# Group 0's feed-forward in 512 columns, and one DRAM array for a head's queries, keys and decay rows

## The chip, the cores and the metric

The kernel runs on one core of a Trainium2 chip. The metric is device microseconds of one launch, the median of several runs. TensorE (PE in the profile) multiplies, with weight loads as a row of their own (PEld); VectorE (DVE), ScalarE (ACT) and GpSimd (POOL) do the elementwise work; SyncE (SP) issues nearly all DMA transfers, which run on the core's 16 DMA engines.

## The reference

One layer of a streaming encoder, for a prompt of 1024 frames and a running stream of 32 frames ("the sample"), D = 1024, all float32. Cut to what matters:

```python
h = x * (1 + sc1) + sh1                                  # modulated input, mod = silu(c) @ w_ada + b_ada
mq, mk, mv, mo, mi, mf, fq, fk, fv, ff, gu, gv = split(h @ w_in)
hm = mlstm(mq, mk, mv, li, lf)                           # 4 heads of 64, in chunks
logits = fq @ fk.T * 64**-0.5 + F[t] - F[s]              # fox: 8 heads of 64, F = cumsum(log_sigmoid(ff)), causal
hf = softmax(logits) @ fv
hg = gu * (tril(ws) @ layer_norm(gv) + bs)               # spatial gate, chunks of 128
x = layer_norm(ALPHA * x + (1 + g1) * (concat(hm, hf, hg) @ w_o))
h = x * (1 + sc2) + sh2
y = (silu(h @ w_gate) * (h @ w_up)) @ w_down             # feed-forward, 2816 wide
x = layer_norm(ALPHA * x + (1 + g2) * y)
```

The outputs are x, the fox keys, values and log-forgets, the mLSTM states and the sample's normed gv. The sample's fox attention also runs over 256 cached rows.

## The kernel before

Activations lie transposed, features on the partitions and frames in the free dimension. The 1056 frames make two groups: group 0 is frames 0 to 511, group 1 the other 512 and the 32 of the sample (544 columns). Each large product is done with both operands split into a high float32r part and a low rest: `gemm` issues three matmuls for each 128x128 block of weights (high x high, high x low, low x high). `weights` loads a block of 512 KB to `raw` (three buffers), rounds it on ACT to `whi` and subtracts on DVE to `wlo`.

`MM` cuts each group in two: 256 + 256 columns, and 272 + 272. `up(c, j, ...)` makes one of 22 blocks of 128 hidden features: for each cut, 24 matmuls for the gate and 24 for the up weights, SiLU, and the split into `acth` and `actl`. `down(c, g, ...)` adds a group of three or four such blocks (`GROUPS`) to the residual `z`; for each cut and each of 8 output blocks it runs 3 matmuls a hidden block and then `sublayer_end` on DVE. The layer-norm input to `up` lies in `hh` and `hl`, one tile a cut, made by `operand`.

The fox heads: `evac_qk(h)` takes the projection of one head, 64 query rows above 64 key rows, and stores its high and low parts to the DRAM arrays `dqh` and `dql`, [8, 128, 1056] each, once for each range of 256 or 272 columns. `gates` stores rows for the decay to `dfs` (8 partitions of 6 rows, 8 times). `fox(h, chunks)` then loads for one head `qp` (queries, high over low), `k1` (the high keys twice), `q2` (high queries over four decay rows), `k2` (low keys over four decay rows) and `v`, with nine loads:

```python
self.load(f(qp[0:64]), self.dqh[h, 0:64, qs])
self.load(f(qp[64:128]), self.dql[h, 0:64, qs])
self.load(f(k1[0:64]), self.dqh[h, 64:128, :nk])
self.load(f(k1[64:128]), self.dqh[h, 64:128, :nk])
...
```

`fox_chunk` takes query tiles of 128: two accumulating matmuls a bank of scores (`qp` with `k1`, `q2` with `k2`), maximum, exponential, division; then for each key block it transposes the probabilities to a PSUM bank, copies them to `pth` on ACT, subtracts to `ptl` on DVE, and multiplies both with `v`. `foxbufs` gives the number of buffers of `k1`, of `qp` and `q2`, of `k2` and of `v`: (2, 1, 1, 2) for group 0 and (2, 1, 1, 1) for group 1.

The order: projections with the fox heads and mLSTM blocks of group 0 between them (`ORDER`), the spatial gate, the output product and layer norm of group 0, the queries and keys of group 1 for the later heads, then `mixers` (fox on group 1 with query tiles 4 to 7, five mLSTM blocks after the heads of `MLB`, and the sample's fox at head `SAMP`), group 0's feed-forward, group 1's output product, and group 1's feed-forward, most of whose blocks run in `sup` with seven smaller products for eight. The program is written in that order, but a planner puts the instructions of each engine in order with a model of their times: it weaves the feed-forward of group 0 between the heads of `mixers`. On the chip each engine runs its own instructions strictly in the planned order.

Of the kernel before, what the change touches and what calls it, by code (L numbers as in the profile page):

```python
# [10 lines left out]
ALU = mybir.AluOpType  # L11
# [16 lines left out]
LN = MM  # L28
GROUPS = ((0, 3), (3, 3), (6, 4), (10, 4), (14, 4), (18, 4))
# [8 lines left out]
SAMP = 7  # L38
MLB = (1, 3, 5, 6, 7)
# [30 lines left out]
class Kernel:  # L70
# [288 lines left out]
    def evac_qk(self, h):  # L359
        nc = self.nc  # L360

        def evac(o, n, ps):
# [6 lines left out]
            self.store(self.dqh[h, :, o:o + n], f(hi[:, :n]))  # L369
            self.store(self.dql[h, :, o:o + n], f(lo[:, :n]))  # L370
# [15 lines left out]
    def gates(self):  # L386
# [47 lines left out]
        for j in range(8):  # L434
# [7 lines left out]
            self.store(self.dfs[:, :, j * P:(j + 1) * P], f(fr[64:72]))  # L442
# [214 lines left out]
    def fox(self, h, chunks):  # L657
# [26 lines left out]
    def fox_chunk(self, h, tiles, W, nq, k1, k2, qp, q2, v):  # L684
        nc, mx = self.nc, self.mx
        nb = tiles[-1] + 1
        t = lambda shape, dt, tag, bufs: self.t(mx, shape, dt, tag, bufs)
        probs = []
# [33 lines left out]

        o = self.t(self.po, [P, 512], F32, "o")
        full = tiles[0] + 1
        order = [0] + list(range(full, nb)) + list(range(1, full))
        held = None
        for x, b in enumerate(order):
            first = max(0, b - tiles[0])
            ps = self.t(self.pt, [P, 512], F32, "t")
            lo = first * P  # L730
            for y in range(first, len(tiles)):
                nc.tensor.transpose(ps[:, y * P:(y + 1) * P], probs[y][:, b * P:(b + 1) * P], self.ident)  # L732
            ph = t([P, max(nq, 384)], F32R, "pth", 3)
            pl = t([P, nq], F32R, "ptl", 2)
            nc.scalar.copy(ph[:, lo:nq], ps[:, lo:nq])  # L735
            nc.vector.tensor_tensor(pl[:, lo:nq], ps[:, lo:nq], f(ph[:, lo:nq]), ALU.subtract)  # L736
            nc.tensor.matmul(o[:, :nq] if b == 0 else o[0:64, lo:nq], v[:, b, :] if b == 0 else v[:, b, 0:64],
                             pl[:, lo:nq], start=b == 0, stop=False)
            if b == 0 and full == 1:
                held = ph  # L740
            else:
                nc.tensor.matmul(o[:, lo:nq], v[:, b, :], ph[:, lo:nq], start=False, stop=full > 1 and x == nb - 1)
            yield
            self.phase = "fox"
# [11 lines left out]
    def fox_sample(self):  # L756
# [29 lines left out]
        for g in range(2):  # L786
# [22 lines left out]
            pT = t([P, 3, P], "pth", 3)  # L809
# [81 lines left out]
    def operand(self, c, pool):  # L891

        new = lambda tag, n: self.t(pool, [P, KT * 272], F32R, tag, 1)[:, :KT * n].rearrange("p (k n) -> p k n", k=KT)
        self.hh[c], self.hl[c] = ({a: new(f"{x}{a}", b - a) for a, b in MM[c]} for x in ("ah", "al"))

    def wo_mix(self, c, ks):
        self.phase = f"wo{c}"
        nc = self.nc
        for a, b in MM[c]:
            for k in ks:  # L900
                r = self.t(self.p2, [P, 272], F32, "tmp", 4)[:, :b - a]
                self.load(r, self.dmix[c][:, k, a:b])
                nc.scalar.copy(self.hh[c][a][:, k], r)
                nc.vector.tensor_tensor(self.hl[c][a][:, k], r, f(self.hh[c][a][:, k]), ALU.subtract)
# [6 lines left out]
    def wo(self, c, st, cuts, eng, res=None):  # L911
# [6 lines left out]
        for m in range(KT):  # L918
# [5 lines left out]
            if m == 0:  # L924
                for i in range(KT):
                    for p, (a, b) in zip(ps, cuts):
                        self.gemm(p[:, :b - a], w[i:i + 1], slice(0, P), lambda _: hh[a][:, ko[i]],
                                  lambda _: hl[a][:, ko[i]], start=i == 0, stop=i == KT - 1)
            for p, (a, b) in zip(ps, cuts):
                if m:  # L930
                    self.gemm(p[:, :b - a], w, slice(0, P), lambda i: hh[a][:, ko[i]], lambda i: hl[a][:, ko[i]])
# [20 lines left out]
    def ln1(self, c, st, a, b):  # L952
# [3 lines left out]
        for k in range(KT):  # L956
# [11 lines left out]
            nc.scalar.copy(hh[:, k], h)  # L968
# [582 lines left out]
```

## Time and profile before

| | us |
|---|---|
| median of 3 runs (lowest, highest) | 1403.94 (1403.85, 1404.99) |
| the profiled execution, its own time | 1406.04 |
| its span, from the first to the last instruction | 1404.3 |
| PE busy / PEld busy | 1360.3 / 1310.1 |
| DVE busy / ACT busy / POOL busy | 1042.7 / 657.6 / 258.2 |

Busy times of PE are modelled, since matmuls are pipelined: the distance between starts tells more than the length of one. A line such as `L117 PE MATMUL up_g<-wo_ah,up_whi` names the line of the kernel (a helper's, here `gemm`), the engine, and the tiles written and read; the first part of a name is the phase in which the tile was made. `start_dqh` is the array `dqh`; `fox_k` stands for `k1` and `k2`, and `fox_q` for `q2`. The DMA share is the mean over the 16 DMA engines; it does not tell one from another.

### The profile page before, as it was taken

The numbers are of one execution on the slowest core, as the hardware profiler recorded it, in microseconds if no ns is written. First come the engines' busy times: TensorE is split into PE (matmuls) and PEld (weight loads), VectorE is DVE, ScalarE is ACT, GpSimd is POOL, SyncE is SP. The second block draws the span as 40 slices with busy tenths as digits, with TensorE's granted clock in tenths as the row PEclk, the third lists the DMA queues.
The fourth block names the chain that finished last, engine by engine and source line by source line (L and its number), as shares of the span: only waits on it lengthen the run. The fifth ranks groups of instructions, "written<-read, shape, count | busy, mean of one in ns | idle before, by whom it ended". The sixth has DMA issues, their size and how long they took to land.

```text
span 1404.3 us, 28827 instructions
## 1 busy us (share of the span) xinstructions
PE 1360.3 (97%) x10933; PEld 1310.1 (93%) x10933; DVE 1042.7 (74%) x2370; ACT 657.6 (47%) x1394; POOL 258.2 (18%) x299
## 2 busy tenths in 40 slices
PE   7999999999999899999999999999999999999996
PEld 4899988989889789999999999999999999999996
DVE  5548655668778768787787775577998989788777
ACT  3323234434445555555545454244663644445355
POOL 0103200042256600000000000353620000000331
PEclk9999999999999999999999999999999999999998
DMA  9754678475654576345443433655497667553321
GB/s 361 252 216 133 188 215 249 147 234 152 209 192 158 173 215 184 106 122 151 128 118 112 122 84 99 154 160 136 156 242 217 187 186 202 147 173 107 105 91 64
DMA packets 136386, 233.28 MB, mean 166 GB/s; under 512 B 22564, under 2 KB 79532, under 8 KB 136248
## 3 DMA queue, kind: packets, MB, share of 16 engines
q1 hardware_dynamic: 130936, 221.34, 50.5%
q0 software_dynamic: 5168, 9.96, 4.6%
q8 instruction: 86, 1.41, 0.4%
q14 instruction: 52, 0.43, 0.1%
q10 hardware_dynamic: 144, 0.14, 0.0%
HBM read 197.50 MB, written 53.81 MB: 179 GB/s over the span
## 4 chain that ended last, share of the span: by engine, by line
PE 81%; DMA 7%; DVE 7%; ACT 2%; issue 1%; SPq 1%; POOL 1%; DVEq 0%; ACTq 0%; POOLq 0%
PE up_g L118 5%; PE up_g L119 5%; PE up_g L117 5%; PE dn_g L117 4%; PE dn_g L118 4%; PE dn_g L119 4%; PE tm_g L282 3%; PE tm_g L283 3%; PE tm_g L284 3%; PE sup_u L119 3%; PE sup_u L117 3%; PE sup_u L118 3%; PE fox_t L732 2%; PE wo_g L118 2%; PE fm_g L117 2%; PE wo_g L117 2%
## 5 line engine op out<-in xcount | busy, mean ns | idle before, releaser
L117 PE MATMUL up_g<-wo_ah,up_whi 128*128 128x256 f32 (+1 forms) x704 | 200.6, 286 | 4.1 <-ACT lna_tmp L964 3.4
L118 PE MATMUL up_g<-wo_al,up_whi 128*128 128x256 f32 (+1 forms) x704 | 202.4, 288 | 0.6 <-DVE wo_al L969 0.6
L119 PE MATMUL up_g<-wo_ah,up_wlo 128*128 128x256 f32 (+1 forms) x704 | 200.9, 286 | 0.0
L117 PEld LDWEIGHTS up_g<-wo_ah,up_whi 128*128 128x128 f32 x704 | 133.3, 190 | 5.6 <-ACT lna_tmp L964 3.5
L118 PEld LDWEIGHTS up_g<-wo_al,up_whi 128*128 128x128 f32 x704 | 133.4, 190 | 1.4 <-DVE wo_al L969 0.8
L119 PEld LDWEIGHTS up_g<-wo_ah,up_wlo 128*128 128x128 f32 x704 | 133.6, 190 | 0.4 <-DVE up_wlo L106 0.2
L283 PE MATMUL tm_g<-tm_wlo,start_h1h 128*128 128x256 f32 (+1 forms) x384 | 111.2, 290 | 0.0
L284 PE MATMUL tm_g<-tm_whi,start_h1l 128*128 128x256 f32 (+1 forms) x384 | 110.9, 290 | 0.0
L282 PE MATMUL tm_g<-tm_whi,start_h1h 128*128 128x256 f32 (+1 forms) x384 | 110.3, 289 | 0.2 <-ACT tm_mixs L633 0.2
L117 PE MATMUL fm_g<-start_h1h,fm_whi 128*128 128x256 f32 (+2 forms) x344 | 101.9, 301 | 6.1 <-DVE fm_qkl L367 2.5
L118 PE MATMUL fm_g<-start_h1l,fm_whi 128*128 128x256 f32 (+2 forms) x344 | 101.8, 296 | 0.5 <-DVE start_h1l L223 0.5
L119 PE MATMUL fm_g<-start_h1h,fm_wlo 128*128 128x256 f32 (+2 forms) x344 | 100.8, 294 | 0.0
L117 PE MATMUL dn_g<-up_acth,dn_whi 128*128 128x256 f32 (+1 forms) x344 | 100.5, 293 | 0.0
L1088 ACT CAST sup_whi<-sup_raw 128x1024 fp32r<-128x1024 f32 x54 | 56.0, 1048 | 91.4 <-PE dn_u L118 47.8
L118 PE MATMUL dn_g<-up_actl,dn_whi 128*128 128x256 f32 (+1 forms) x344 | 98.7, 287 | 0.0
L119 PE MATMUL dn_g<-up_acth,dn_wlo 128*128 128x256 f32 (+1 forms) x344 | 98.5, 286 | 0.0
L735 ACT CAST fox_pth<-fox_t 128x256 fp32r<-128x256 f32 (+3 forms) x144 | 51.0, 373 | 65.7 <-PE fox_t L732 62.1
L1089 DVE TENSOR_TENSOR sup_wlo<-sup_raw,sup_whi 128x1024 fp32r<-128x1024 f32 x54 | 68.0, 1263 | 10.7 <-ACT sup_whi L1088 10.7
L282 PEld LDWEIGHTS tm_g<-tm_whi,start_h1h 128*128 128x128 f32 x384 | 73.5, 192 | 2.6 <-issue 1.6
L117 PEld LDWEIGHTS fm_g<-start_h1h,fm_whi 128*128 128x128 f32 x344 | 65.4, 192 | 11.3 <-DVE fm_qkl L367 3.2
L106 DVE TENSOR_TENSOR up_wlo<-up_raw,up_whi 128x1024 fp32r<-128x1024 f32 x50 | 63.3, 1265 | 16.5 <-ACT up_whi L105 16.2
L736 DVE TENSOR_TENSOR fox_ptl<-fox_t,fox_pth 128x256 fp32r<-128x256 f32 (+3 forms) x144 | 58.1, 417 | 22.6 <-ACT fox_pth L735 21.3
(577 smaller groups left out, 4678.9 us busy)
## 6 DMA issues: line engine op xcount, KB each, us to landing
up_raw<-w_gu SPq DMA_DIRECT2D x50, 512.0 KB
dn_raw<-w_dn SPq DMA_DIRECT2D x28, 512.0 KB
ada_late<-w_ada SPq DMA_DIRECT2D x24, 512.0 KB
wo_raw<-w_o SPq DMA_DIRECT2D x24, 512.0 KB
sup_raw<-w_gu SPq DMA_DIRECT2D x20, 512.0 KB
start_dp<-w_gu SPq DMA_DIRECT2D x19, 512.0 KB
start_dp<-w_gu POOLq DMA_DIRECT2D x19, 512.0 KB, 8.1
sup_raw<-start_dp SPq DMA_DIRECT2D x18, 512.0 KB
```

The lines of the kernel that those rows point to most:

```text
L106: (eng or nc.vector).tensor_tensor(lo[:, :w], raw[:, :w], f(hi[:, :w]), ALU.subtract)
L117: nc.tensor.matmul(ps, hi, xh(k), start=start and k == 0, stop=False)
L118: nc.tensor.matmul(ps, hi, xl(k), start=False, stop=False)
L119: nc.tensor.matmul(ps, lo, xh(k), start=False, stop=stop and k == n - 1)
L282: nc.tensor.matmul(ps[:, :ncol], xh, hi, start=k == 0, stop=False)
L283: nc.tensor.matmul(ps[:, :ncol], xh, lo, start=False, stop=False)
L284: nc.tensor.matmul(ps[:, :ncol], xl, hi, start=False, stop=k == 7)
L732: nc.tensor.transpose(ps[:, y * P:(y + 1) * P], probs[y][:, b * P:(b + 1) * P], self.ident)
L735: nc.scalar.copy(ph[:, lo:nq], ps[:, lo:nq])
L736: nc.vector.tensor_tensor(pl[:, lo:nq], ps[:, lo:nq], f(ph[:, lo:nq]), ALU.subtract)
L1088: nc.scalar.copy(h, x)
L1089: tt(l, x, f(h), ALU.subtract)
```

## The change

- Queries, keys and decay rows of a head go to one array `dq`, [8, 2, 2, 68, 1056]: head; queries or keys; high or low; 64 rows and four decay rows. `evac_qk` stores as before two transfers a range, and `gates` two where it stored one. `fox` loads `qp` in one transfer, `k1` in one (a broadcast), `q2` in one and `k2` in one, and `v`.
- `up` runs 512 columns at once for j = 1 to 17 of group 0, `down` for its first five groups. The operand of group 0 is one tile of 512 columns; the views for the cuts are taken from it.
- `fox_chunk` puts two key blocks in one bank, so that one copy and one subtraction serve both.
- `mixers` runs the sample's fox first, and weaves each mLSTM block with a head at half its pace; `MLB` is (1, 2, 3, 4, 5).

```diff
+WIDE = ((0, 512),)
...
-SAMP = 7
-MLB = (1, 3, 5, 6, 7)
+MLB = (1, 2, 3, 4, 5)
...
-            self.store(self.dqh[h, :, o:o + n], f(hi[:, :n]))
-            self.store(self.dql[h, :, o:o + n], f(lo[:, :n]))
+            for i, x in enumerate((hi, lo)):
+                self.store(self.dq[h, :, i, 0:64, o:o + n], f(x[:, :n]))
...
-            self.store(self.dfs[:, :, j * P:(j + 1) * P], f(fr[64:72]))
+            self.store(self.dq[:, 1, 1, 64:68, j * P:(j + 1) * P], f(fr[64:72, 0:4]))
+            self.store(self.dq[:, 0, 0, 64:68, j * P:(j + 1) * P], f(fr[64:72, 2:6]))
...
-        self.load(f(qp[0:64]), self.dqh[h, 0:64, qs])
-        self.load(f(qp[64:128]), self.dql[h, 0:64, qs])
-        self.load(f(k1[0:64]), self.dqh[h, 64:128, :nk])
-        self.load(f(k1[64:128]), self.dqh[h, 64:128, :nk])
-        self.load(f(q2[0:64]), self.dqh[h, 0:64, qs])
-        self.load(f(q2[64:68]), self.dfs[h, 2:6, qs])
-        self.load(f(k2[0:64]), self.dql[h, 64:128, :nk])
-        self.load(f(k2[64:68]), self.dfs[h, 0:4, :nk])
+        self.load(f(qp), self.dq[h, 0, :, 0:64, qs])
+        self.load(f(k1), self.dq[h, 1, 0:1, 0:64, :nk].to_broadcast([2, 64, nk]))
+        self.load(f(q2), self.dq[h, 0, 0, :, qs])
+        self.load(f(k2), self.dq[h, 1, 1, :, :nk])
         self.load(f(v), self.dv[:, :nb, h * P:(h + 1) * P])
...
+        units = [order[x:x + 2] for x in range(0, nb, 2)] if full > 1 else [[0], [1], [2, 3]]
...
-        for x, b in enumerate(order):
-            first = max(0, b - tiles[0])
+        for unit in units:
             ps = self.t(self.pt, [P, 512], F32, "t")
-            lo = first * P
-            for y in range(first, len(tiles)):
-                nc.tensor.transpose(ps[:, y * P:(y + 1) * P], probs[y][:, b * P:(b + 1) * P], self.ident)
-            ph = t([P, max(nq, 384)], F32R, "pth", 3)
-            pl = t([P, nq], F32R, "ptl", 2)
-            nc.scalar.copy(ph[:, lo:nq], ps[:, lo:nq])
-            nc.vector.tensor_tensor(pl[:, lo:nq], ps[:, lo:nq], f(ph[:, lo:nq]), ALU.subtract)
...
+            at, e = [], 0
+            for b in unit:
...
+                at.append((b, slice(e, e + w), slice(first * P, nq)))
+                e += w
+            ph = t([P, 512], F32R, "pth", b5)
+            pl = t([P, 512], F32R, "ptl", 2)
+            nc.scalar.copy(ph[:, :e], ps[:, :e])
+            nc.vector.tensor_tensor(pl[:, :e], ps[:, :e], f(ph[:, :e]), ALU.subtract)
+            for b, c, q in at:
...
     def operand(self, c, pool):
 
+        if c == 0:
+            if 0 not in self.hh:
+                tile = lambda tag: self.t(pool, [P, KT * 544], F32R, tag, 1)[:, :KT * 512].rearrange(
+                    "p (k n) -> p k n", k=KT)
+                self.hh[0], self.hl[0] = ({0: x, 256: x[:, :, 256:]} for x in (tile("ah"), tile("al")))
+            return
...
     def mixers(self):
+        def slow(part):
+            for _ in part:
+                yield
+                yield
+
+        self.fox_sample()
         for h in range(8):
-            weave(self.fox(h, ((4, 5), (6, 7))))
-            if h == SAMP:
-                self.fox_sample()
+            parts = [self.fox(h, ((4, 5), (6, 7)))]
             if h in MLB:
-                weave(self.mlstm(self.nextm))
+                parts.append(slow(self.mlstm(self.nextm)))
                 self.nextm += 1
+            weave(*parts)
...
-        self.dqh = t([8, P, T], "dqh")
-        self.dql = t([8, P, T], "dql")
+        self.dq = t([8, 2, 2, 68, T], "dq")
...
-        self.foxbufs = (2, 1, 1, 2)
+        self.foxbufs = (2, 1, 1, 2, 3)
...
-        self.foxbufs = (2, 1, 1, 1)
+        self.foxbufs = (2, 1, 1, 1, 2)
...
-                weave(self.up(0, j, act, pa, MM[0]))
+                weave(self.up(0, j, act, pa, WIDE if 0 < j < GROUPS[-1][0] else MM[0]))
...
-                self.down(0, g, act, MM[0], st)
+                self.down(0, g, act, WIDE, st)
             else:
-                self.down(0, g, act, MM[0])
+                self.down(0, g, act, WIDE)
```

More of the change, by code (lines that the diff above doesn't have):

```diff
@@ L687, in fox_chunk @@
         t = lambda shape, dt, tag, bufs: self.t(mx, shape, dt, tag, bufs)
+        b5 = self.foxbufs[4]
         probs = []
@@ L725, in fox_chunk @@
         order = [0] + list(range(full, nb)) + list(range(1, full))
+        units = [order[x:x + 2] for x in range(0, nb, 2)] if full > 1 else [[0], [1], [2, 3]]
         held = None
[L727 to L728 removed]
+        for unit in units:
             ps = self.t(self.pt, [P, 512], F32, "t")
[L730 to L742 removed]
+            at, e = [], 0
+            for b in unit:
+                first = max(0, b - tiles[0])
+                w = nq - first * P
+                for y in range(first, len(tiles)):
+                    c = e + (y - first) * P
+                    nc.tensor.transpose(ps[:, c:c + P], probs[y][:, b * P:(b + 1) * P], self.ident)
+                at.append((b, slice(e, e + w), slice(first * P, nq)))
[5 more added lines that the diff above has]
+            for b, c, q in at:
+                nc.tensor.matmul(o[:, q] if b == 0 else o[0:64, q], v[:, b, :] if b == 0 else v[:, b, 0:64],
+                                 pl[:, c], start=b == 0, stop=False)
+                if b == 0 and full == 1:
+                    held = ph
+                else:
+                    nc.tensor.matmul(o[:, q], v[:, b, :], ph[:, c], start=False, stop=full > 1 and b == order[-1])
             yield
```

25 lines of the change are left out of this document (13 added, 12 removed).

## The prediction

> **What bounds the kernel now.** I read the page's busy times and slices first, then its DMA queue row, then busy times by stage. The page:
>
> ```profile
> span 1404.3 us, 28827 instructions
> PE 1360.3 (97%) x10933; PEld 1310.1 (93%) x10933; DVE 1042.7 (74%) x2370; ACT 657.6 (47%) x1394; POOL 258.2 (18%) x299
> ...
> DMA  9754678475654576345443433655497667553321
> GB/s 361 252 216 133 188 215 249 147 234 152 209 192 158 173 215 184 106 122 151 128 118 112 122 84 99 154 160 136 156 242 217 187 186 202 147 173 107 105 91 64
> ...
> q1 hardware_dynamic: 130936, 221.34, 50.5%
> ```
>
> TensorE is busy 97% of the span, so the kernel is bound by its instruction stream; the next engine, DVE, has a quarter free. The queue row gives the price of a byte on one DMA engine: 221.34 MB in 50.5% of 16 engines' 1404.3 us is 19.5 KB/us for one engine. The first slice, DMA at nine tenths or more and 361 GB/s, gives 361/16 = 22.6 KB/us when all are full. I use 19.5 and 22.6 as the two ends.
>
> By stage (columns: length, then busy us and instructions of PE, PEld, DVE, ACT, POOL, granted clock, DMA share, GB/s):
>
> ```profile
> 120.00:490.00 370.00, 349.77 (x2804) 328.59 (x2803) 260.90 (x657) 161.21 (x375) 118.33 (x136) 0.98 0.61 186
> 490.00:895.00 405.00, 404.88 (x3330) 395.07 (x3329) 294.25 (x752) 208.68 (x515) 9.10 (x17) 0.99 0.46 128
> ```
>
> 120 to 490 holds the projections, the forgetting-attention (fox) heads on group 0 and the gates; 490 to 895 is the fox heads on group 1, woven by the planner into group 0's feed-forward. In the second stage TensorE is never idle: a step taken off DVE, ACT or SP there wins nothing, and only fewer or cheaper matmuls shorten it. The DMA engines are mean 61% and 46% busy, that is 226 us and 186 us each: room, if it is shared evenly.
>
> **Wide feed-forward.** `up` runs 512 columns at once for j = 1 to 17 (`WIDE if 0 < j < GROUPS[-1][0]`), `down` for groups 0 to 4 (18 blocks). Pairs of 256-wide matmuls that become one of 512: 17 x 2 x 8 x 3 = 816 and 18 x 8 x 3 = 432, in sum 1248. TensorE's timeline, a run of 512-wide ones and a run of 256-wide ones (start, modelled length; starts count):
>
> ```profile
> 42.61 0.39 PE L118 MATMUL fm_g<-start_h1l,fm_whi 128*128 128x512 f32 x1
> ...
> 43.53 0.27 PE L185 MATMUL ada_t<-start_ident,ada_adas 128*128 128x128 f32 x1
> ...
> 543.71 0.28 PE L118 MATMUL dn_g<-up_actl,dn_whi 128*128 128x256 f32 x1
> ...
> 544.66 0.27 PE L732 MATMUL fox_t<-start_ident,fox_p 128*128 128x128 f32 x1
> ```
>
> Four 512-wide matmuls take 43.53 - 42.61 = 0.92 us, 230 ns each; eight 256-wide ones 0.95 us, 119 ns each. A pair saves 8 ns, and 1248 pairs about 9 us. All of it lies on TensorE in a stage that TensorE bounds, so it counts in full. Between 5 us (the starts are rounded to 10 ns) and 10 us.
>
> The Trainium skill (TensorE: Matmul & The Clock Gate, Back-to-back issue gap) gives N/2.4 + 2.5 ns for an isolated warm matmul; by that a pair would save 2.5 ns and the sum would be 3 us instead of 9. The trace's 119 and 230 ns both lie above that rule's 109 and 216.
>
> **Fox evacuations and the mixers' order.** Transposed blocks are now copied two to a bank: 8 x 3 + 8 x 7 = 80 copies and 80 subtractions instead of 144 each.
>
> ```profile
> L735 ACT CAST fox_pth<-fox_t x144: 263/372/592, 184.8 to 849.9; 128x256 fp32r<-128x256 f32 x104, 128x128 fp32r<-128x128 f32 x24, 128x512 fp32r<-128x512 f32 x8, 128x384 fp32r<-128x384 f32 x8
> L736 DVE TENSOR_TENSOR fox_ptl<-fox_t,fox_pth x144: 265/417/693, 185.4 to 850.3; 128x256 fp32r<-128x256 f32 x104, 128x128 fp32r<-128x128 f32 x24, 128x512 fp32r<-128x512 f32 x8, 128x384 fp32r<-128x384 f32 x8
> ```
>
> A 512-wide copy takes at most 592 ns against two of 372, a subtraction 693 against two of 417: some 0.15 us a pair on ACT and DVE, both with a quarter or more free in either stage. I cost it at nothing; feed-forward matmuls cover it, and without that cover it would bring at most 64 x 0.3 = 19 us. Weaving the mLSTM blocks into the heads and putting the sample's attention first only reorders work that the same matmuls already hide: nothing, with a few us either way at the stage's ends. The doubled width of SiLU and of the residual steps is hidden in the same way.
>
> **The DRAM array, fewer loads.** Four DMA issues a head go. SP, around the second group-1 head, and that head's first score matmuls:
>
> ```profile
> 514.99 0.47 SPq L87 DMA_DIRECT2D fox_qp<-start_dqh  x1
> ...
> 517.69 0.49 SPq L87 DMA_DIRECT2D fox_q<-start_dfs  x1
> 518.22 0.45 SPq L87 DMA_DIRECT2D fox_k<-start_dql  x1
> ...
> 519.23 1.08 SPq L87 DMA_DIRECT2D fox_k<-start_dqh  x2
> ```
>
> ```profile
> 522.11 0.44 PE L701 MATMUL fox_s<-fox_k,fox_qp 128*128 128x384 f32 x1
> ...
> 523.02 0.45 PE L702 MATMUL fox_s<-fox_k,fox_q 68*128 68x384 f32 x1
> ```
>
> An issue is about half a us, so 16 x 4 x 0.5 = 32 us leave SP's queue. SP waits for buffers anyway, and TensorE is full: nothing, at most the 2 us by which a head's loads start earlier.
>
> What matters is the shape. Before, each load or store of queries and keys had 64 or 128 rows as its outermost dimension. After, the DRAM side is [2, 64, n] for `qp` and `k1` and for both stores of `evac_qk`, and 68 rows for `q2` and `k2`. Where the outermost dimension is what a transfer is shared out by, 2 rows reach 2 engines and 68 rows reach 4 (the largest count up to 16 that divides it). No row of before has a transfer with an outermost 2, so both ends are open: 16 engines (cost nothing) and 2.
>
> The Trainium skill (DMA: Bandwidth & Descriptors, Why a DMA increments its semaphore by 16 and not by 1) states such a sharing: the slowest dimension that isn't 1 is taken of either side, and the largest number of engines up to 16 that divides both. As far as the trace goes it agrees: in its records of completion steps, which no view prints, a 64-row load of a head posts 16 steps and the decay store of `gates`, 48 rows from 8 partitions, only 9.
>
> Bytes, from the DMA issues:
>
> ```profile
> start_dqh<-fm_qkh SPq DMA_DIRECT2D x16, 136.0 KB
> start_dql<-fm_qkl SPq DMA_DIRECT2D x16, 136.0 KB
> ...
> start_dqh<-fm_qkh SPq DMA_DIRECT2D x16, 128.0 KB
> start_dql<-fm_qkl SPq DMA_DIRECT2D x16, 128.0 KB
> fox_qp<-start_dqh SPq DMA_DIRECT2D x16, 128.0 KB
> fox_qp<-start_dql SPq DMA_DIRECT2D x16, 128.0 KB
> ...
> fox_k<-start_dqh SPq DMA_DIRECT2D x16, 256.0 KB
> ...
> fox_k<-start_dqh SPq DMA_DIRECT2D x16, 128.0 KB
> fox_q<-start_dqh SPq DMA_DIRECT2D x16, 128.0 KB
> ...
> fox_k<-start_dql SPq DMA_DIRECT2D x8, 256.0 KB
> ...
> fox_k<-start_dql SPq DMA_DIRECT2D x8, 128.0 KB
> ```
>
> Stores: 32 x 136 + 32 x 128 = 8448 KB. On 16 engines 0.54 MB each; on two 4.33 MB each, so these two carry 3.79 MB more: 168 us at 22.6, 194 us at 19.5. Nearly all issue inside the first stage:
>
> ```profile
> L91 SPq DMA_DIRECT2D start_dqh<-fm_qkh x32: 319/382/1739, 109.5 to 474.8; - x32
> ```
>
> Group-0 loads, a head: `qp` 256 and `k1` 256 KB on two engines, `q2` and `k2` 136 KB each on four, 324 KB on the busiest instead of 49: 282 KB (in thousands of bytes) more, 8 heads 2.25 MB, 100 to 115 us. Group-1 loads, a head: 256 + 512 KB on two, 136 + 272 on four, 486 KB instead of 74: 422 thousand bytes more, 8 heads 3.38 MB, 149 to 173 us.
>
> First stage: 226 + 168 + 100 = 494 us at the one end, 226 + 194 + 115 = 535 at the other, for the two busiest engines, in a stage of 370. Weight loads are spread over all engines and need these two as well, so the stage overflows by 124 to 165 us. Second stage: 186 + 149 to 173 is 335 to 359 of 405 us: 46 to 70 us are free, and part of the overflow (keys of late heads) can fall there. I take 120 us for the first stage.
>
> In the second stage each head waits longer for its own loads. In the rows above the first matmul follows its load's issue by 7.1 us and the second by 4.8 us. On two engines `qp` alone takes 262 thousand bytes/2/22.6 = 5.8 us, `q2` 1.5 and `k2` 3.1 after it; with the 2.6 us that a transfer between issue and use takes in the chain below, the second matmul can start at 515.0 + 10.4 + 2.6 = 528.0 instead of 523.0: 5 us later. TensorE runs in order, so the feed-forward matmuls queued behind it stand too: 8 x 5 = 40 us. The first head's `k1` is not fetched a head ahead: 524 thousand bytes/2/22.6 = 11.6 us instead of 1.4, another 10. I take 50 us.
>
> An existing wait grows: SP holds a head's loads until its store has landed, with weight loads queued behind it. The chain of waits shows this:
>
> ```profile
> 236.64 2.62 DMA start_dqh<-fm_qkh
> 239.34 0.45 SPq L87
> 239.83 3.43 DMA fox_k<-start_dqh
> ```
>
> Those 2.62 us become over 6 for the two stores of a range, and weight loads behind them start later. That is inside the 120 us.
>
> **Sum**, on the profiled execution's span of 1404.3 us (its own time lies 1.7 us above, the median 0.3 below): 1404 - 9 + 120 + 50 = 1565 us.
>
> **Rivals.** (1) The transfers are spread as evenly as before, because the outermost 2 is not what they are shared by. Then only the wide matmuls count: 1404 - 9, less a us for earlier loads: 1394. For it: DMA shares of 0.61 and 0.46, and no row that shows a two-engine transfer. It decides against me if `fox_s` waits no longer than the 7.1 us above. (2) Two engines carry them, but prefetched weights and the free 39% of the first stage take the overflow, and only a head's own latency is left: 16 x 5 - 9 = 71, or 1475 us. Against it: 494 us don't fit 370. (3) No overflow is absorbed and every group-1 head stands for all its extra transfer: 165 + 173 - 9, or 1733 us. Against it: `k1` has two buffers and is fetched a head ahead (its loads are issued at 519, behind `k2`, for the next head).
>
> **How the numbers follow.** Forecast 0.64, (1) 0.16, (2) 0.16, (3) 0.04. I prefer the two-engine end because 2 and 68 are outermost as the code writes them and strides of 68 rows leave nothing to merge. The forecast's own range: first stage 54 (the least overflow, less all of the free 70) to 165, latency 30 (four heads that wait 5, and the first one's 10) to 130 (three quarters of the 173 that all extra group-1 loads take), so 1480 to 1690. With (2), and some room below its 1475, the range is 1430 to 1690, which leaves out (1) and (3), 2 in 10. A measurement tells about 0.2%, 2.8 us, from no change. Faster 0.14 and same 0.02 come from (1), whose gain could shrink to 3 us; slower 0.84 is the rest.
>
> **What would show it.** Right: TensorE's share falls below 90%, with idle time before `fox_s` (L701, L702 of before) put down to the new loads in 120 to 490; matmuls fall by 1248 to about 9685, and 512-wide `up_g` keeps 230 ns; DMA share in that stage is not near 1 although TensorE waits, since fourteen engines idle. Wrong: `fox_s` waits as before and the first stage keeps its 370 us; then rival 1 holds. If 512-wide matmuls start 238 ns apart, the 9 us are gone.

## The result: 17% slower, and where the time went

The changed kernel takes 1646.66 us (median of six runs, 1642.04 to 1649.19), the kernel before 1404.38 beside it: a ratio of 1.1729, with an interval of 1.1708 to 1.1751. The forecast was 1565 us, the range 1430 to 1690. The page of the changed kernel, those lines that answer to the ones shown of before:

```profile
span 1640.3 us, 25912 instructions
PE 1408.8 (86%) x9683; PEld 1284.2 (78%) x9683; DVE 1033.7 (63%) x2214; ACT 640.4 (39%) x1261; POOL 260.5 (16%) x292
...
PEclk9997887869699897879999998999999999999999
DMA  9642443425346453443334333423645957754321
...
PE 55%; DMA 25%; DVE 7%; issue 6%; SPq 3%; ACT 2%; POOL 1%; ACTq 0%; DVEq 0%; POOLq 0%
...
L699 PE MATMUL fox_s<-fox_k,fox_qp 128*128 128x384 f32 (+2 forms) x96 | 38.2, 413 | 112.5 <-DMA fox_qp<-start_dq 74.8
```

Of before, the chain and the same group of score matmuls:

```profile
PE 81%; DMA 7%; DVE 7%; ACT 2%; issue 1%; SPq 1%; POOL 1%; DVEq 0%; ACTq 0%; POOLq 0%
...
L701 PE MATMUL fox_s<-fox_k,fox_qp 128*128 128x384 f32 (+2 forms) x96 | 33.8, 364 | 4.9 <-DMA fox_k<-start_dqh 3.5 <-DMA fox_qp<-start_dql 1.3 <-issue 0.2
```

The span grew by 236 us, but TensorE is busy only 48.5 us longer; its share falls from 97% to 86%. In the row `DMA` nine of the first twenty slices were at six tenths or more; now three are, and eleven of the same slices of `PEclk` show a granted clock of six to eight tenths. The DMA engines carry less at a time, and TensorE waits: the chain is now a quarter DMA, 7% before, and ahead of the group of first score matmuls (`fox_s` line: busy us, mean ns, then the idle time ahead of it and what ended most of that) TensorE stood idle for 112.5 us, 74.8 of them until `qp` had landed. Before, it was 4.9 us in all.

By stage (columns as before):

```profile
120.00:490.00 370.00, 249.63 (x1781) 229.41 (x1782) 152.44 (x432) 87.13 (x221) 45.76 (x61) 0.82 0.38 119
490.00:895.00 405.00, 332.59 (x2003) 285.49 (x2003) 235.47 (x501) 158.06 (x323) 74.93 (x83) 0.90 0.44 132
```

In 120 to 490 us TensorE is busy for 250 us instead of 350, at a granted clock of 0.82 instead of 0.98, while the DMA engines' mean share falls from 0.61 to 0.38. This fits a few engines that work and many that idle; the share is a mean and does not show it engine by engine.

The chain that ended last shows how long one transfer takes. Some of its DMA pieces (start, us, what), before, then after:

```profile
287.43 5.76 DMA start_dql<-fm_qkl
...
294.38 3.12 DMA fox_k<-start_dql
...
460.57 3.86 DMA start_dql<-fm_qkl
```

```profile
112.64 11.31 DMA start_dq<-fm_qkl
...
197.70 14.79 DMA fox_k<-start_dq
...
247.77 12.07 DMA fox_k<-start_dq
...
398.65 10.08 DMA start_dq<-fm_qkl
...
608.88 8.01 DMA start_dq<-fm_qkl
...
687.95 21.80 DMA fox_q<-start_dq
...
800.39 19.25 DMA fox_k<-start_dq
...
856.28 21.96 DMA fox_k<-start_dq
```

A store of a range's low parts, 5.8 and 3.9 us in the chain of before, now holds it for 8 to 11 us; a head's keys, 3.1 us before, in the pieces shown for 12 to 22, and the queries `q2` of the first group-1 head for 21.8. The views of single tiles (instruction, count: shortest/median/longest issue in ns) show that SP itself is held up, for tiles that the change does not touch too. Before (weights, `q2`), then after:

```profile
L87 SPq DMA_DIRECT2D up_raw<-w_gu x50: 327/333/609, 441.0 to 1020.2; - x50
```

```profile
L87 SPq DMA_DIRECT2D fox_q<-start_dqh x16: 540/546/1498, 163.3 to 770.0; - x16
```

```profile
L87 SPq DMA_DIRECT2D up_raw<-w_gu x50: 327/333/6521, 594.7 to 1255.9; - x50
```

```profile
L87 SPq DMA_DIRECT2D fox_q<-start_dq x16: 437/488/9853, 186.1 to 1072.2; - x16
```

The median issue of a weight load is unchanged, but the longest grew from 0.6 to 6.5 us, and that of `q2` from 1.5 to 9.9. What stands behind such an issue on SP's queue starts later by as much.

The waits also cost clock. The same 344 and 384 matmuls of two projections, busy us and mean ns of one by line; before, then after:

```profile
L284 PE MATMUL tm_g<-tm_whi,start_h1l 128*128 128x256 f32 (+1 forms) x384 | 110.9, 290 | 0.0
...
L119 PE MATMUL fm_g<-start_h1h,fm_wlo 128*128 128x256 f32 (+2 forms) x344 | 100.8, 294 | 0.0
```

```profile
L284 PE MATMUL tm_g<-tm_whi,start_h1l 128*128 128x256 f32 (+1 forms) x384 | 115.4, 302 | 0.0
...
L119 PE MATMUL fm_g<-start_h1h,fm_wlo 128*128 128x256 f32 (+2 forms) x344 | 104.6, 305 | 0.0
```

These two lines wait for nothing (idle 0.0) and still take 4% longer, at the lower clock. Each projection has three such groups; the six together are busy for 27 us more (663.9 us instead of 636.9).

One place of the changed kernel's trace shows the cost at full size: TensorE's timeline (start, modelled length; in brackets the idle time ahead), and the stretches around (columns as before):

```profile
708.50 0.66 PE L699 MATMUL fox_s<-fox_k,fox_qp 128*128 128x384 f32 x1 [21.74 <-DMA fox_qp<-start_dq]
...
710.71 0.63 PE L118 MATMUL up_g<-mlstm_al,up_whi 128*128 128x512 f32 x1
...
714.55 0.63 PE L118 MATMUL up_g<-mlstm_al,up_whi 128*128 128x512 f32 x1
...
718.15 0.39 PE L118 MATMUL up_g<-mlstm_al,up_whi 128*128 128x512 f32 x1
...
719.78 0.39 PE L119 MATMUL up_g<-mlstm_ah,up_wlo 128*128 128x512 f32 x1
```

```profile
709.75:715.00 5.25, 5.20 (x14) 4.22 (x14) 1.78 (x5) 1.51 (x3) 0.00 (x0) 0.50 0.08 33
718.00:721.00 3.00, 3.00 (x14) 2.33 (x13) 0.44 (x1) 1.18 (x2) 0.00 (x0) 1.00 0.31 107
```

After 21.7 us of waiting for `qp`, 512-wide matmuls start 427 ns apart at a granted clock of 0.50 (nine distances from 710.71 to 714.55); a few us later they start 233 ns apart at 1.00 (seven from 718.15 to 719.78).

Two landmarks cut the span: the last projection of a fox head's queries and keys (`fm_g`), and the last product of a group-1 head with its values (`fox_o`). They stand as the last start in the views of these tiles. Before and after:

```profile
L119 PE MATMUL fm_g<-start_h1h,fm_wlo x344: 274/287/497, 19.1 to 468.1; 128*128 128x272 f32 x84, 128*128 128x256 f32 x80, 128*128 128x512 f32 x8
```

```profile
L742 PE MATMUL fox_o<-fox_pth,fox_v x136: 271/282/416, 189.3 to 853.1; 128*128 128x256 f32 x104, 128*128 128x128 f32 x24, 128*128 128x384 f32 x8
```

```profile
L119 PE MATMUL fm_g<-start_h1h,fm_wlo x344: 277/287/497, 19.4 to 629.5; 128*128 128x272 f32 x84, 128*128 128x256 f32 x80, 128*128 128x512 f32 x8
```

```profile
L748 PE MATMUL fox_o<-fox_pth,fox_v x136: 272/280/415, 237.6 to 1135.1; 128*128 128x256 f32 x104, 128*128 128x128 f32 x24, 128*128 128x384 f32 x8
```

Up to the first landmark the changed kernel loses 161 us (629.5 against 468.1), between the two another 121 (505.6 against 385.0), and behind the second it is 46 us shorter (505.2 against 551.2). That last part is not a gain of its own, as e6_rows below shows.

### The profile page after: what moved, and what is told of

Same layout as the page of the kernel before. It is cut to its first block, busy times and chain, and to the rows that moved or that the text cites. A ratio compares the mean times of both kernels' runs of the same rounds, so it can differ in the third digit from the quotient of the medians.

```text
span 1640.3 us, 25912 instructions
## 1 busy us (share of the span) xinstructions
PE 1408.8 (86%) x9683; PEld 1284.2 (78%) x9683; DVE 1033.7 (63%) x2214; ACT 640.4 (39%) x1261; POOL 260.5 (16%) x292
## 4 chain that ended last, share of the span: by engine, by line
PE 55%; DMA 25%; DVE 7%; issue 6%; SPq 3%; ACT 2%; POOL 1%; ACTq 0%; DVEq 0%; POOLq 0%
DMA fox_k<-start_dq 6%; PE up_g L117 4%; PE up_g L118 3%; PE up_g L119 3%; DMA start_dq<-fm_qkl 3%; PE dn_g L117 3%; PE dn_g L119 3%; PE dn_g L118 3%; SPq L87 3%; PE sup_u L119 2%; PE sup_u L117 2%; PE sup_u L118 2%; DMA up_raw<-w_gu 2%; DMA wo_tmp<-start_dmix 2%; PE wo_g L117 2%
## 5 line engine op out<-in xcount | busy, mean ns | idle before, releaser
L117 PE MATMUL up_g<-mlstm_ah,up_whi 128*128 128x512 f32 (+1 forms) x384 | 146.6, 382 | 8.2 <-DVE fm_qkl L367 7.7
L118 PE MATMUL up_g<-mlstm_al,up_whi 128*128 128x512 f32 (+1 forms) x384 | 146.1, 381 | 0.8 <-DVE mlstm_al L983 0.8
L119 PE MATMUL up_g<-mlstm_ah,up_wlo 128*128 128x512 f32 (+1 forms) x384 | 145.8, 380 | 0.0
L699 PE MATMUL fox_s<-fox_k,fox_qp 128*128 128x384 f32 (+2 forms) x96 | 38.2, 413 | 112.5 <-DMA fox_qp<-start_dq 74.8
L708 ACT ACTIVATE fox_p<-fox_s,fox_fmx 128x384 f32<-128x384 f32 (+2 forms) x96 | 55.0, 578 | 111.7 <-DVE fox_fmx L703 76.7
L105 ACT CAST up_whi<-up_raw 128x1024 fp32r<-128x1024 f32 x50 | 52.4, 1048 | 113.8 <-DMA up_raw<-w_gu 74.6
L117 PEld LDWEIGHTS up_g<-mlstm_ah,up_whi 128*128 128x128 f32 x384 | 76.8, 200 | 22.0 <-DVE fm_qkl L367 5.9
L118 PEld LDWEIGHTS up_g<-mlstm_al,up_whi 128*128 128x128 f32 x384 | 77.4, 202 | 13.3 <-DVE mlstm_al L983 0.9
L119 PEld LDWEIGHTS up_g<-mlstm_ah,up_wlo 128*128 128x128 f32 x384 | 77.1, 201 | 11.7
L703 DVE TENSOR_REDUCE fox_fmx<-fox_s 128x1 f32<-128x384 f32 (+2 forms) x96 | 52.5, 552 | 49.9 <-PE fox_s L700 48.9
L284 PEld LDWEIGHTS tm_g<-tm_whi,start_h1l 128*128 128x128 f32 x384 | 78.8, 206 | 1.0 <-issue 0.8
```

Of the source, the lines that this page charges most:

```text
L105: nc.scalar.copy(hi[:, :w], raw[:, :w])
L117: nc.tensor.matmul(ps, hi, xh(k), start=start and k == 0, stop=False)
L118: nc.tensor.matmul(ps, hi, xl(k), start=False, stop=False)
L119: nc.tensor.matmul(ps, lo, xh(k), start=False, stop=stop and k == n - 1)
L284: nc.tensor.matmul(ps[:, :ncol], xl, hi, start=False, stop=k == 7)
L699: nc.tensor.matmul(s[:, :w], qp[:, qc], k1[:, lo:hi], start=True, stop=False)
```

## The experiments

My theory: the array's transfers are shared out by their outermost size, 2 or 68, and so run on two or four of the 16 DMA engines; the other parts of the change are worth a few us. Rivals: one array for all of it is what costs (layout, dependences, order on SP); the fox copies and the order of the mixers cost or bring something of their own; the bytes overflow a stage, or else each head's own wait counts.

| kernel | what it is | median us | ratio to before (interval) |
|---|---|---|---|
| e2_array | before + the array, its stores and five loads | 1658.02 | 1.1806 (1.1788 to 1.1824) |
| after | the whole change | 1646.66 | 1.1729 (1.1708 to 1.1751) |
| e8_order | e6_rows, `qp` and `k1` loaded with outermost 2 | 1516.88 | 1.0805 (1.0779 to 1.0830) |
| e9_pad | e6_rows, stores with outermost 2 | 1503.47 | 1.0705 (1.0678 to 1.0732) |
| e7_wide | before + 512 columns | 1460.71 | 1.0397 (1.0380 to 1.0413) |
| e12_weave | e7_wide + new order of the mixers | 1437.53 | 1.0234 (1.0209 to 1.0258) |
| e11_units | e7_wide + fox copies two to a bank | 1428.60 | 1.0170 (1.0148 to 1.0191) |
| e1_pieces | after, its transfers in pieces of 64 and 4 rows | 1421.92 | 1.0133 (1.0105 to 1.0162) |
| e13_narrow | e6_rows with 256 columns | 1414.69 | 1.0079 (1.0051 to 1.0107) |
| e6_rows | after, the array laid out as [8, 128, 2, 1056] | 1405.34 | 1.0012 (0.9998 to 1.0026) |
| e15_best | e3_rest, sample behind the last head | 1405.28 | 1.0005 (0.9991 to 1.0019) |
| e14_late | e6_rows, sample behind the last head | 1400.02 | 0.9971 (0.9955 to 0.9987) |
| e3_rest | the change without the array | 1395.70 | 0.9931 (0.9910 to 0.9953) |

A thousandth is 1.4 us; differences below are taken between ratios.

**e2_array**: the array alone, in the kernel before.

```
-self.dqh = t([8, P, T], "dqh"); self.dql = t([8, P, T], "dql"); self.dfs = t([8, 6, S], "dfs")
+self.dq = t([8, 2, 2, 68, T], "dq")
 ... (stores of evac_qk and gates, loads of fox as in the change; all else as before)
```

> The kernel before with the one array and its five loads and two stores alone; feed-forward, fox copies and the order of the mixers as before. Sharing: 1640 to 1660 us, the changed kernel's time plus the 5 to 10 us of the wide matmuls. One array: the same 1640 to 1660 us. Order: 1404 us, since the order is that of before.

It loses 253.6 us. With the rest of the change around it the array costs as much: 1.1729 - 0.9931 of e3_rest, 252 us. So the array's stores and loads are all of the loss, in the old order of the mixers as in the new one.

**e1_pieces**: the changed kernel, each transfer cut so that its outermost size is 64 or 4; the same bytes and the same array.

```
-self.store(self.dq[h, :, i, 0:64, o:o + n], f(x[:, :n]))
+for y in range(2):
+    self.store(self.dq[h, y, i, 0:64, o:o + n], f(x[64 * y:64 * y + 64, :n]))
 ...
-self.load(f(qp), self.dq[h, 0, :, 0:64, qs])
+for y in range(2):
+    self.load(f(qp[64 * y:64 * y + 64]), self.dq[h, 0, y, 0:64, qs])
 ... (k1 alike; q2 and k2 in 64 and 4 rows)
```

> The changed kernel with its one array, but every transfer whose outermost dimension is 2 or 68 is issued in pieces of 64 (or 4) rows: four stores a range instead of two, nine loads a head instead of five. Sharing (a transfer of outermost 2 runs on two DMA engines, one of 68 on four): all of the loss goes, 1396 to 1400 us, since only the 512-wide matmuls (1248 pairs at 4 to 8 ns) are left. One array (loads of a head wait for stores of others into the same array): stays near 1640 us. Order (the new order of the mixers or the shared banks of fox cost the time): stays near 1640 us.

Of 17.3% only 1.3% is left. The array and the program's order are the same, and only the outermost size and the number of issues were changed, so the rival "one array" falls. The planner's order on the engines is not the same: it differs from kernel to kernel. But the six kernels with spread transfers and no dip (this one, e6_rows, e13_narrow, e14_late, e15_best, e3_rest) all lie between 0.7% below and 1.3% above before, and those with an outermost 2 are 7% or more above it: the loss goes with the outermost size, not with one order. The 17 us above e6_rows were not expected. They show in the first stage, where most of the 64 additional stores are issued, and two more loads a head; the stage's row of e1_pieces, then of e6_rows:

```profile
120.00:490.00 370.00, 340.93 (x2685) 320.83 (x2684) 242.24 (x611) 148.22 (x338) 100.33 (x119) 0.96 0.59 175
```

```profile
120.00:490.00 370.00, 347.26 (x2797) 326.95 (x2796) 262.45 (x649) 157.17 (x364) 117.70 (x137) 0.98 0.62 187
```

TensorE does 112 matmuls less in it. That issues cost nothing is in doubt here, but the order differs too, and no run took the stores apart from the loads.

**e6_rows**: the high and low parts of a row side by side, so that one transfer has the outermost size 128; the decay rows in their own array as before; seven loads, two stores a range.

```
-self.dq = t([8, 2, 2, 68, T], "dq")
+self.dq = t([8, P, 2, T], "dq")
 ...
-self.load(f(qp), self.dq[h, 0, :, 0:64, qs])
-self.load(f(k1), self.dq[h, 1, 0:1, 0:64, :nk].to_broadcast([2, 64, nk]))
+self.load(f(qp), self.dq[h, 0:64, :, qs].rearrange("r i n -> (r i) n"))
+self.load(f(k1), self.dq[h, 64:128, 0:1, :nk].to_broadcast([64, 2, nk]))
```

> The changed kernel with the array laid out as [8 heads, 128 rows, high or low, columns], so that the outermost dimension is 128 in the stores and in the load of qp and 64 in that of k1 (the partitions of qp and k1 then alternate high and low in the same way, which leaves their product as it is); q2 and k2 take 64 rows from it and four decay rows from an array as before: seven loads a head, two stores a range. Sharing: 1394 to 1400 us, as with the pieces, since fewer issues win nothing. One array: near 1640 us. If issues matter: some us below the kernel in pieces.

All of the loss is gone, and no gain is left: the same time as before, 5 us above the upper end of what was expected.

**e8_order** and **e9_pad** put the outermost 2 back, first into two loads, then into the stores, with the bytes and the issues of e6_rows.

```
 e8_order
-self.dq[h, 0:64, :, qs].rearrange("r i n -> (r i) n")
+self.dq[h, 0:64, :, qs].rearrange("r i n -> i r n")     # k1 alike
 e9_pad
-self.dq = t([8, P, 2, T], "dq")
+self.dq = t([8, 2, 65, 2, T], "dq")                     # a spare row: two halves that don't merge
```

> Like e6_rows, with the same bytes and the same seven loads a head, but qp and k1 are read with the outermost size 2 (high and low rows by halves) instead of 128 and 64; stores and the small loads are left spread. Sharing by the outermost size says: qp and k1 alone go through two engines, 230 thousand bytes more on the busiest for a group-0 head and 344 for a group-1 head, 81 to 94 us and 122 to 141 us in all; 226 + 81 to 94 fits the 370 us of the first stage and 186 + 122 to 141 fits the 405 of the second, so nothing overflows and only each head's own longer wait is left: 50 to 110 us more than e6_rows, 1455 to 1515 us. If overflow doesn't count and each transfer's wait does, the loads have most of the 241 us between e6_rows and the changed kernel: over 1540. Had e6_rows won by its partition order or by its array's layout, this kernel stays within 5 us of 1405.

> Like e6_rows, with one unused row behind every 64, so that a store of 128 partitions has the outermost size 2; loads stay at 128 and 64. Sharing by the outermost size says: 8448 KB of stores on two engines, 168 to 194 us more on these; 226 + 168 to 194 is 394 to 420 of the 370 us of the first stage, an overflow of 24 to 50 us, and a longer wait of each head's loads behind its store, 16 ranges of 4 us at most: 30 to 110 us more than e6_rows, 1435 to 1515, all of it before 490 us or just behind it. With e8_order the two sum to less than the 241 us of the changed kernel if only together they overflow (60 us less or more); to 241 within 20 us if each wait counts by itself. Had the layout no part in it, 1405.

The loads cost 111 us, the stores 97, together 209 of the 241 us between e6_rows and the changed kernel; 32 are left to the transfers on four engines, to the decay stores and to what the two do to each other. That is neither of the two sums expected (60 or more less, or within 20). By the bytes, either kernel would have had little or no overflow. The landmarks of e6_rows, e8_order, e9_pad, in this order:

```profile
L119 PE MATMUL fm_g<-start_h1h,fm_wlo x344: 274/286/796, 19.6 to 468.2; 128*128 128x272 f32 x84, 128*128 128x256 f32 x80, 128*128 128x512 f32 x8
```

```profile
L749 PE MATMUL fox_o<-fox_pth,fox_v x136: 272/280/342, 189.2 to 898.7; 128*128 128x256 f32 x104, 128*128 128x128 f32 x24, 128*128 128x384 f32 x8
```

```profile
L119 PE MATMUL fm_g<-start_h1h,fm_wlo x344: 277/287/501, 19.1 to 528.4; 128*128 128x272 f32 x84, 128*128 128x256 f32 x80, 128*128 128x512 f32 x8
```

```profile
L749 PE MATMUL fox_o<-fox_pth,fox_v x136: 272/281/416, 204.5 to 1008.1; 128*128 128x256 f32 x104, 128*128 128x128 f32 x24, 128*128 128x384 f32 x8
```

```profile
L119 PE MATMUL fm_g<-start_h1h,fm_wlo x344: 278/287/498, 19.2 to 552.5; 128*128 128x272 f32 x84, 128*128 128x256 f32 x80, 128*128 128x512 f32 x8
```

```profile
L749 PE MATMUL fox_o<-fox_pth,fox_v x136: 271/280/341, 214.8 to 993.7; 128*128 128x256 f32 x104, 128*128 128x128 f32 x24, 128*128 128x384 f32 x8
```

Against e6_rows, with the spans of the profiled executions (1402.9, 1513.3, 1499.1, 1640.3):

| | to the last `fm_g` | from there to the last `fox_o` | behind it |
|---|---|---|---|
| two-engine loads (e8_order) | +60 | +49 | +1 |
| two-engine stores (e9_pad) | +84 | +11 | +1 |
| the changed kernel | +161 | +75 | +1 |

e9_pad lies in its range, and 84 of its 97 us are lost ahead of the last `fm_g`, as expected. e8_order lies just above the upper end of what a head's own longer wait was to cost, and loses 60 us in the first stage, where by the bytes two engines had 50 us or more to spare. What counts is therefore not only whether the two engines are full over a stage. The likely reason, argued and not measured by itself, is that each transfer takes long, a head's loads stand behind its stores, and SP and TensorE stand behind these in order. By waits, TensorE stood 49.8 us before `fox_s` for `qp` in e8_order, 3.2 us in e6_rows (second line):

```profile
L700 PE MATMUL fox_s<-fox_k,fox_qp 128*128 128x384 f32 (+2 forms) x96 | 38.7, 415 | 79.2 <-DMA fox_qp<-start_dq 49.8 <-ACT fox_p L709 12.0 <-issue 9.7
```

```profile
L700 PE MATMUL fox_s<-fox_k,fox_qp 128*128 128x384 f32 (+2 forms) x96 | 34.2, 368 | 5.5 <-DMA fox_qp<-start_dq 3.2 <-ACT fox_p L709 1.4 <-DMA fox_k<-start_dq 0.8
```

**e7_wide**: the 512 columns alone.

```
+WIDE = ((0, 512),)
 ...
-weave(self.up(0, j, act, pa, MM[0]))
+weave(self.up(0, j, act, pa, WIDE if 0 < j < GROUPS[-1][0] else MM[0]))
 ... (operand, down and the tiles as in the change; array, fox_chunk and mixers as before)
```

> The kernel before with the 512-column feed-forward of group 0 alone. By the prediction's 8 ns a pair: 1395 us, 9 us less than before. By the changed kernel's trace, whose 512-wide matmuls start 233 ns apart against 2 x 118.5 ns: 1248 x 4 ns = 5 us less, 1399 us. If the wider feed-forward starves the banks: 1404 us or more.

Neither gain came: it loses 56 us. That is "1404 us or more", but what the trace shows is one dip, not starved banks all along the feed-forward. Its slices, its last `fox_o`, and 880 to 980 us in e7_wide and in before:

```profile
PE   7999999999999899999999995679999999999996
...
PEclk9999999999999999999999997579999999999998
```

```profile
L743 PE MATMUL fox_o<-fox_pth,fox_v x136: 271/281/416, 190.4 to 920.7; 128*128 128x256 f32 x104, 128*128 128x128 f32 x24, 128*128 128x384 f32 x8
```

```profile
880.00:980.00 100.00, 60.62 (x318) 47.90 (x317) 53.48 (x129) 27.51 (x80) 18.54 (x17) 0.64 0.23 70
```

```profile
880.00:980.00 100.00, 99.68 (x789) 98.41 (x790) 68.18 (x123) 36.67 (x75) 40.78 (x47) 0.98 0.59 152
```

The feed-forward that the planner puts between the steps of the fox heads is used up before the heads end (last `fox_o` at 920.7 us, 853.1 before); no matmul of the feed-forward starts between 873 and 948 us:

```profile
873.19 0.28 PE L120 MATMUL up_g<-mlstm_ah,up_wlo 128*128 128x256 f32 x1
...
947.71 0.55 PE L118 MATMUL up_u<-mlstm_ah,up_whi 128*128 128x256 f32 x1 [1.38 <-DVE fm_Cs L591]
```

The chain of small steps runs bare there, and TensorE is busy 61 of the 100 us from 880 at a clock of 0.64. Why the heads end later is argued, not measured by itself: each of their steps waits behind blocks of feed-forward twice as long.

**e11_units** and **e12_weave** add one of the other two parts to e7_wide.

```
 e11_units
+units = [order[x:x + 2] for x in range(0, nb, 2)] if full > 1 else [[0], [1], [2, 3]]
 ... (fox_chunk as in the change; mixers as before)
 e12_weave
+self.fox_sample()
 for h in range(8):
+    parts = [self.fox(h, ((4, 5), (6, 7)))]
+    if h in MLB:
+        parts.append(slow(self.mlstm(self.nextm)))
 ... (mixers as in the change; fox_chunk as before)
```

> e7_wide (512 columns alone, 1460.7 us) with the fox copies two to a bank, old order of the mixers. Theory a: a head is a chain of steps, each waiting behind the feed-forward matmuls queued ahead of it, which are twice as long in 512 columns; half as many steps restore it: 1395 to 1412 us, the last fox_o before 870 us. Theory b: the new order (recurrent mixer woven with a head at half pace, sample first) is what fills the heads' time: then this kernel stays at 1440 to 1465 us with the dip at 886 to 965 us. If each gives a part, 1412 to 1440.

> e7_wide with the new order of the mixers alone (sample first, the recurrent mixer woven with a head at half pace), a key block to a bank as before. Theory a (number of steps of a head): 1440 to 1465 us, fox_o still ends near 920 us. Theory b (weaving): 1395 to 1412. If each gives a part, 1412 to 1440.

Each gives a part, the third case: 32 us the copies, 23 the order, and both (e3_rest) 65. The same 100 us, of e11_units, e12_weave and e3_rest:

```profile
880.00:980.00 100.00, 80.11 (x559) 72.63 (x558) 59.07 (x103) 30.64 (x67) 36.20 (x34) 0.81 0.43 125
```

```profile
880.00:980.00 100.00, 88.80 (x537) 77.58 (x536) 70.14 (x131) 41.28 (x102) 31.25 (x29) 0.88 0.43 127
```

```profile
880.00:980.00 100.00, 100.00 (x750) 96.65 (x749) 75.14 (x123) 47.06 (x94) 49.77 (x48) 1.00 0.59 170
```

From 61 us of TensorE to 80, 89 and 100: the dip closes. In e12_weave the last `fox_o` is even later than in e7_wide (932.7 us), so what matters is that feed-forward and heads end together.

**e13_narrow** and **e3_rest** ask what the parts are worth the other way round.

```
 e13_narrow (against e6_rows)
-WIDE = ((0, 512),)
+WIDE = MM[0]
 e3_rest (against the change)
-self.dq = t([8, 2, 2, 68, T], "dq")
+self.dqh = t([8, P, T], "dqh"); self.dql = t([8, P, T], "dql"); self.dfs = t([8, 6, S], "dfs")
 ... (their nine loads and their stores as before)
```

> e6_rows with the feed-forward of group 0 in 256 columns again: the fox copies two to a bank, the new order of the mixers and the spread transfers remain. If the copies and the order only make up for the longer matmuls queued ahead of each step of a head, they are worth nothing without these: before has 30.5 us of waits over 0.6 us in all, and 1396 to 1406 us result. If they save 23 and 32 us by themselves (what e12_weave and e11_units gained over e7_wide), about 1350. If wide matmuls give their 9 us in e6_rows, this kernel is 9 us slower than e6_rows, 1414.

> The change without the array: 512 columns, fox copies, order of the mixers; queries and keys in the old two arrays and the decay rows in their own, nine loads a head. Against e6_rows it differs by two loads a head (32 issues on SP) and by where qp and k1 have their rows. If an issue costs nothing where SP has room, 1402 to 1408 us, within 3 us of e6_rows; if each costs its part of a microsecond on the path, up to 16 us more.

Without wide matmuls the copies and the order bring no gain: e13_narrow is 0.8% slower than before. It has the array of e6_rows too, so the 0.8% need not be theirs; before with these two parts alone was not run. It is 0.67% slower than e6_rows, 9.4 us (5 to 14 by the two intervals): there the wide matmuls give what the forecast gave them. e3_rest, with all three parts, is 0.69% faster than before, 9.7 us, and with that the best version run. But the expectation that it equals e6_rows failed: it is 0.8% faster than this, though it issues two loads a head more. One load in place of two brought nothing; whether it costs these 0.8%, or the layout of the array or the planner's order does, was not tried.

**e14_late** and **e15_best** put the sample's attention behind the last head again, in e6_rows and in e3_rest.

```
-self.fox_sample()
 for h in range(8):
     ...
     weave(*parts)
+self.fox_sample()
```

> e6_rows with the sample rows' attention behind the last head, as before, instead of ahead of the first. It waited 2.4 us at 485 us in e6_rows and keeps the first head of group 1 from starting until 514 us (489.5 before). If that start is what eats the 9 us of the wide matmuls, 1394 to 1402 us. If the sample behind the last head has no feed-forward left beside it, as in e7_wide, 1405 to 1425.

> e3_rest (the change without the array) with the sample rows' attention behind the last head, as before: what helped e6_rows (e14_late, 5 us) put together with what helped more (the old arrays, 10 us). If the early sample's wait for its own loads costs here too, 1389 to 1393 us. If the two gains have one source (the first head of group 1 starting late behind the sample's loads, 508.7 us in e3_rest and 514.0 in e6_rows), 1394 to 1398, no better than e3_rest.

In e6_rows it gains 0.4%, as the first case had it; in e3_rest it loses 0.7%, which neither had. So it is not the early sample as such that costs. What decides between these neighbours of some 10 us was not found: the orders of all engines differ a little from one to the other.

## Why the prediction was right, and where it was not

**Two and four engines: right.** `qp` on two engines was the first thing to look for, and `fox_s` waits for it 74.8 us; the DMA share in the first stage is far from 1. In the records of completion steps, which no view prints, `qp` and the stores post 3 steps and the 68-row loads 5, where the 64-row loads of before post 16. That is one step more than the two and four engines of the theory. In e8_order `qp` and `k1` post 3 and the stores 16, in e9_pad the stores post 3 and `qp` and `k1` 16, in e6_rows all of them 16. What settles that the outermost size costs the time is e1_pieces and e6_rows, which change it and lose the loss, and e8_order and e9_pad, which bring it back in part. The Trainium skill (DMA: Bandwidth & Descriptors, Rules for kernel authors) says that an outermost dimension below 16 confines a transfer to so many engines at most; e8_order and e9_pad agree, slower by 8% and 7%.

**Its price: too low, and by the wrong sum.** The step that failed is the overflow: the two engines' bytes against the length of a stage, less what is free. It gave 120 us for the first stage, and a head's latency 50 for the second; 161 and 75 were lost. That 161 lies within the 124 to 165 us by which the bytes overflowed is no proof of the step. By it the loads alone fit both stages and cost a head's latency only, 50 to 110 us; e8_order measured 111, 60 of them in the stage where nothing overflows. By it the stores alone overflow by 24 to 50 us; in e9_pad the first stage lost 84. So waits of single transfers cost time in the first stage beyond the overflow, where the prediction put them inside its 120 us. It was partly luck that the time stayed in the range: the wide ends, not the mechanism, took in the missing 81 us. The term for the two stores of a range was "over 6" us, where the chain shows 8 to 11; the loads ahead of the second matmul of a group-1 head were to take 10.4 us together, where the chain has 19 us for `k2` of a later head alone (the piece at 800.39). And nothing was put in for the clock: granted 0.82 instead of 0.98 in the first stage, in which TensorE waited most. The Trainium skill (TensorE: Matmul & The Clock Gate, What's actually happening) says that the clock falls to half after about 3.4 us of idle; the trace agrees: 427 ns instead of 233 behind a wait of 21.7 us.

**Wide feed-forward: about right in size, not on its own.** 9 us were forecast and 9.4 (5 to 14) measured, e13_narrow against e6_rows, with 9683 matmuls where about 9685 were to be seen. The price of a pair does not hold as well: 233 ns apart at full clock, not 230, saves 5 ns against two of 119, which makes 6 us of 1248 pairs; the measured time does not tell 6 from 9. The 3 us that the sum would have as an estimate by the Trainium skill (TensorE: Matmul & The Clock Gate, Back-to-back issue gap) lie below the 5 to 14 that were measured. And the sentence "it counts in full" holds only with the next part.

**Fox copies and mixers' order at "nothing": wrong.** Their cover was named, the feed-forward matmuls, and what they cost without it: at most 19 us. Not asked was whether the wide matmuls leave the cover as it was. e7_wide, e11_units and e12_weave show that they do not: without these two parts the wide feed-forward loses 56 us, not gains 9. The three belong together. That their sum came out right, 9.7 us for all three in e3_rest, is luck: one error took away what the other gave.

**Fewer issues at "nothing": borne out for fewer, in doubt for more.** e6_rows with two loads a head less than e3_rest gains nothing by it. e1_pieces, with more issues than e6_rows, is 17 us slower, for a reason that stays open.

The sum by what was measured: 1404 - 10 for the three parts, + 252 for the array, is 1646; the 252 is itself the difference between the changed kernel and e3_rest. Of the rivals, the even spread (1394) comes near what is measured once transfers are spread: 1405.3 with one array (e6_rows), 1395.7 with the old ones (e3_rest). Neither latency alone (1475) nor full waits (1733) gives the measured time: the first stage lost nearly the 165 us of the latter, the second 75 of its 173.

## What to carry to other kernels

Before two transfers are merged into one, look at the outermost size of the new one: from 64 or 128 rows to 2 it cost 17% here, and the same merge with the small dimension inside cost at most 0.8%, though it gained nothing either. Two engines that by the bytes are not full over a stage can still set its time (60 us in e8_order): look at how long each transfer takes, and who waits for it. Larger units of filler between a chain of small steps must be paid for with fewer steps, or the filler runs out before the chain does: test such parts together and apart.

## What the hardware showed

That waits cost twice was new here: matmuls with nothing to wait for took 4% longer in the changed kernel (290 to 302 ns, 294 to 305), at a mean granted clock of 0.927 over the span instead of 0.990. And an issue on SP, 0.3 to 0.5 us at the median, took up to 9.9 us for `q2` and 6.5 for a weight load while queries and keys went over two to four engines; the longest before were 1.5 and 0.6. A single long issue proves little: one of 2.8 us stands in e12_weave too, where all these transfers are spread.
